# Hybrid convolution and retention layer on one core: the row factors are spread to all partitions through a DRAM row instead of by products with a unit matrix

## The chip, the core and the metric

The kernel runs on one core of one Trainium2 chip. The metric is the device time of one execution in microseconds, the median of several runs. The engines are named as the profile names them: PE (TensorE, the products), PEld (its weight loads), DVE (VectorE), ACT (ScalarE), POOL (GpSimd), and SP (SyncE, which here only issues DMAs). Each engine works through its own list of instructions in order and waits on semaphores for the others.

## The reference

One layer takes 2048 rows of 1024 numbers, with 16 learned rows ahead of them. The rows are normalised, projected to eight groups of 512, four of which go through a short gated convolution and four through a chunked retention of four heads; both results are gated, joined and projected back.

```python
def rms_norm(x, g):
    xf = x.astype(jnp.float32)
    y = xf * lax.rsqrt(jnp.mean(xf * xf, axis=-1, keepdims=True) + EPS)
    return (y * g.astype(jnp.float32)).astype(x.dtype)

def mixer_layer(h, norm_g, w_in, conv_w, ret_norm_g, w_out, pos):
    hn = rms_norm(h, norm_g)
    proj = jnp.einsum('bld,de->ble', hn, w_in)
    cx, cb, cc, cg, q, k, v, rg = jnp.split(proj, N_PROJ, axis=-1)
    conv_out = short_conv_branch(cx, cb, cc, conv_w) * jax.nn.silu(cg)
    ...
    ret = head_group_norm(retention_chunkwise(qf, kf, vf), ret_norm_g)
    ret_out = ret.astype(h.dtype) * jax.nn.silu(rg)
    mixed = jnp.concatenate([conv_out, ret_out], axis=-1)
    return h + jnp.einsum('ble,ed->bld', mixed, w_out)
```

The factor of each row, `rsqrt(mean(x*x) + EPS)`, is not multiplied into `x` ahead of the projection. The kernel projects the rows with the gain alone and multiplies the factor, or its square, into the results.

## The kernel before

**Layout.** The projections are computed transposed: output channels stand on the partitions, rows of the sequence in the free dimension. So the factor of a row is needed as a row vector that is the same on all 128 partitions. The sequence is done in two halves of 1024 rows (`for r in range(NR)`), each in two blocks of 512 (`j`). Each half goes through eight units: four convolution groups (numbers 4 to 7) and four heads (0 to 3), in the order of `UNITS`. A unit makes two groups of products. An ordinary one (`quad`, L221) takes seven products of twelve matmuls each (L232) instead of eight, with sums of blocks of the weights (`stationary`, L134, on POOL) and of `x` (`block_sums`, `prepare`). The first group after `x` changes is a plain one (`quad_plain`, L278, matmuls at L289) with no sums. After both halves eight pairs of output tiles follow.

**Two-part numbers.** Every operand of the large products is split (`split`, L107): the high half, rounded, by a cast on ACT (L110; with a scale, L113), and the low half by a subtraction on DVE (L122; with a scale, L114). Three matmuls of 128x512 make one full one: low by high, high by low, high by high. Names like `mh30`, `ml30` are the high and low half of block 3, tile 0; `wh`, `wl` are those of a weight.

**The row factors.** `row_factors(r, f)` (L387) is a generator that loads the rows of half r a second time, untransposed (L363), squares and sums them on ACT (L396), and calls `spread_factors` (L366) once for each block of 512. For half 0 it is run through ahead of the first unit; for half 1 its steps are put between the quads of units 5, 6 and 7 of half 0 (`FACTOR_STEPS`). `spread_factors` takes the factors of 512 rows as `rc`, 128 partitions by 4 (POOL's power at L305), and has `spread` (L317) bring them to all partitions as `rr`, 128 by 512, and their squares as `rr2`. `spread` multiplies a unit matrix by the factors on DVE (L310), which makes four diagonal matrices, and has PE multiply a matrix of ones by them, so that each partition receives the whole row in PSUM; ACT copies it out (L337) and squares it (L339). In half 0 that is one float32 product (L336). In half 1 the factors are split into two parts (DVE L326, L327 and ACT L330, the last for the diagonals of the high part) and two products of the rounded form are added (L332, L333). `rr` and `rr2` are read by the units of the same half, `rc2` (the squares by partition) and `ev` by the heads.

**Queues and order.** All loads and stores but a few stand in one queue, SP's. A DMA is issued when the buffer that it writes is free and what it reads is there; the DMAs behind it wait with it. Weight tiles (`ra`, L487) have eight buffers; `x`, the rows `n`, gates and other half-lived tiles share sixteen (`gen`). The order of the instructions on each engine is not the order of the code: a scheduler orders them with times of its own, so that an edit in one place can change the order far from it, within the bounds that `issue_after` and priorities set. When half 0 ends, the second group of unit 7, the split of the sixteen new `x` tiles (L409, L113, L114) and the plain first group of head 0 of half 1 overlap.

Of the kernel before, what the change touches and what calls it, by code (L numbers as in the profile page):

```python
# [8 lines left out]
F32 = mybir.dt.float32  # L9
F32R = mybir.dt.float32r  # L10
BF16 = mybir.dt.bfloat16
U16 = mybir.dt.uint16
AF = mybir.ActivationFunctionType
ALU = mybir.AluOpType

P = 128
# [6 lines left out]
HB = 512  # L23
NR = 2
BLK = SEQ // NR
CH = HB // P
# [53 lines left out]
def hybrid_trunk(ctx: ExitStack, tc: tile.TileContext, t, out: bass.AP, chunk_decay):  # L80
# [5 lines left out]
    nc = tc.nc  # L86
    x = t["x"]

    const = ctx.enter_context(tc.tile_pool(name="const", bufs=1))
    small = ctx.enter_context(tc.tile_pool(name="small", bufs=2))  # L90
    sb = ctx.enter_context(tc.tile_pool(name="sb", bufs=2))
# [6 lines left out]
    def ps_misc():  # L98
        return ps.tile([P, HB], F32, name="ms", tag="ms", bufs=4)

    def gen(name="g"):
        return sb.tile([P, HB + 16], F32, name=name, tag="g", bufs=GEN)[:, : 2 + HB]
# [18 lines left out]
    def sub(eng, out, a, b):  # L121
        eng.tensor_tensor(out=out, in0=a, in1=b, op=ALU.subtract)  # L122
# [185 lines left out]
    def diagonal(out, col, n):  # L308
        a = col.shape[1]
        nc.vector.tensor_tensor(  # L310
            out=out,
            in0=ident[:n, :n].rearrange("p (a c) -> p a c", a=1).broadcast_to([n, a, n]),
            in1=col.rearrange("p (a c) -> p a c", c=1).broadcast_to([n, a, n]),
            op=ALU.mult,
        )

    def spread(col, n, dst, squares=None, two_part=False):  # L317

        a = col.shape[1]
        diag = sb.tile([P, HB], F32R if two_part else F32, name="rot", tag="rot", bufs=1)  # L320
        diag = diag.rearrange("p (a c) -> p a c", a=CH)[:n, :a, :n]
        rp = ps_misc()
        rows = rp[:, : a * n].rearrange("p (a c) -> p a c", a=a)
        if two_part:
            high, low = (small.tile([P, CH], t, name="ch", tag=f"ch{t}")[:n, :a] for t in (F32R, F32))
            nc.vector.tensor_copy(out=high, in_=col)  # L326
            sub(nc.vector, low, col, high.bitcast(F32))  # L327
            highs = gen("dg")[:, :HB].bitcast(F32R).rearrange("p (a c) -> p a c", a=CH)[:n, :a, :n]
            for c in range(a):
                nc.scalar.mul(highs[:, c], ident[:n, :n], high[:, c : c + 1].bitcast(F32))  # L330
            diagonal(diag, low, n)
            nc.tensor.matmul(rows, ones_r[:n].broadcast_to([n, P]), highs, start=True, stop=False)  # L332
            nc.tensor.matmul(rows, ones_r[:n].broadcast_to([n, P]), diag, start=False, stop=True)  # L333
        else:
            diagonal(diag, col, n)
            nc.tensor.matmul(rows, ones[:n].broadcast_to([n, P]), diag, start=True, stop=True)  # L336
        nc.scalar.copy(out=dst, in_=rp[:, : a * n])  # L337
        if squares is not None:
            nc.scalar.activation(squares, rp[:, : a * n], AF.Square)  # L339

    gain = const.tile([P, KT], F32, name="gain")
    ident = const.tile([P, P], F32, name="ident")
    ones = const.tile([P, 1], F32, name="ones")
    ones_r = const.tile([P, 1], F32R, name="ones_r")
    neg_half = const.tile([P, CH], F32, name="neg_half")
    meta_s = const.tile([P, KT, NMETA], F32, name="meta_s")
    cols = const.tile([P, 3 * NG], F32, name="cols")
# [15 lines left out]
            nc.sync.dma_start(a, x[row : row + P, half * HB : (half + 1) * HB])  # L363
        return tiles

    def spread_factors(ss, rr, rr2, two_part):  # L366


        add(nc.vector, ss[:, 0, :], ss[:, 0, :], ss[:, 1, :])
        rc = small.tile([P, CH], F32, name="rc", tag="rc")  # L370
        v = rsqrt_mean(rc, ss[:, 0, :])
        spread(rc, P, rr, rr2, two_part)
        rc2 = small.tile([P, CH], F32, name="rc2", tag="rc2", bufs=2 * NR)
        nc.vector.tensor_tensor(out=rc2, in0=rc, in1=rc, op=ALU.mult)
        ev = small.tile([P, NG, CH], F32, name="ev", tag="ev", bufs=2 * NR)
        nc.vector.tensor_tensor(
            out=ev,
            in0=eps_col.rearrange("p (h c) -> p h c", c=1).broadcast_to([P, NG, CH]),
            in1=v.rearrange("p (h c) -> p h c", h=1).broadcast_to([P, NG, CH]),
            op=ALU.mult,  # L380
        )
        return rc2, ev

    def row_tile(name, pair):
        return sb.tile([P, BLK], F32, name=name, tag=f"rr{pair}", bufs=2)

    def row_factors(r, f):  # L387

        f.extend([row_tile("rr", r), row_tile("rr2", r), []])
        rows = load_rows(r, 0)  # L390
        yield
        for j in range(2):
            ss = small.tile([P, 2, CH], F32, name="ss", tag="ss")
            for c in range(CH):
                for half, a in enumerate(rows):
                    nc.scalar.activation(a, a, AF.Square, accum_out=ss[:, half, c : c + 1])  # L396
                if j * CH + c + 1 < 2 * CH:
                    rows = load_rows(r, j * CH + c + 1)
                yield
            f[2].append(spread_factors(ss, *(a[:, j * HB : (j + 1) * HB] for a in f[:2]), r > 0))  # L400
            yield

    def gain_of(k):
# [507 lines left out]
    make_identity(nc, ident)  # L911
    nc.gpsimd.memset(ones, 1.0)
    nc.gpsimd.memset(neg_half, -0.5)
    nc.vector.tensor_copy(out=ones_r, in_=ones)
    warm = const.tile([P, P], BF16, name="warm")
    nc.vector.memset(warm, 0.0)
    function = const.tile([P, 1], BF16, name="function")
# [21 lines left out]
    for r in range(NR):  # L939
        f = factors[r]  # L940
# [146 lines left out]
```

## Time and profile before

| | |
|---|---|
| median of 3 runs | 876.3 us (876.18 to 877.04) |
| profiled execution, span from first to last instruction | 874.9 us |
| median of the runs less that span | 1.4 us |
| PE busy | 863.1 us (99%) |
| DVE busy | 717.1 us (82%) |
| ACT busy | 474.8 us (54%) |
| POOL busy | 391.2 us (45%) |
| granted clock of PE, mean | 0.997 |
| moved by DMA | 125.32 MB, 143 GB/s on average |

In a row of the timeline stand the start in us from the span's start, the duration in us, the engine, the line of the kernel, the operation, the tiles that it writes and reads, their shapes, and, in brackets, the idle time before it with what ended it. Consecutive instructions of one kind are put together with their count. A row of the groups has count, then busy time in us and the mean of one in ns, then the idle time ahead of the group's instructions. In the rows of the queues stand KB each and the us from issue to landing. Matmuls are pipelined, so that their durations overlap and the distance of two starts is what one takes. Their shapes read "128*128 128x512": the stationary tile and the moving one.

### The profile page before, as it was taken

What the parts mean: (1) busy time and instruction counts of PE and PEld (TensorE: products, weight loads), DVE (VectorE), ACT (ScalarE), POOL (GpSimd) and SP (SyncE); (2) the same over time, 40 slices, a digit from 0 to 9 for tenths busy, and PEclk for the clock granted to TensorE, in tenths of its full rate; (3) what the DMA queues carried; (4) which work ended last, traced back from release to release, by engine and by line L of the source; (5) the groups of instructions that cost most, each with busy time, mean ns of one, the idle gap of its engine ahead of it and who ended that gap; (6) DMA issues with size and microseconds to landing.
All of it is one profiled execution on the core that took longest, in us unless ns stands there. A gap on an engine that the chain in (4) does not pass through costs nothing.

```text
span 874.9 us, 12767 instructions
## 1 busy us (share of the span) xinstructions
PE 863.1 (99%) x4280; PEld 711.8 (81%) x4280; DVE 717.1 (82%) x1190; ACT 474.8 (54%) x883; POOL 391.2 (45%) x286
## 2 busy tenths in 40 slices
PE   8999999999999999999999999999999999999996
PEld 5878788878888778888888888888888888788885
DVE  6889898989887887989889898988767799656664
ACT  8675547374644654846464646444333465545553
POOL 0662332333235555352232333354646545678763
PEclk9999999999999999999999999999999999999998
DMA  9723235353556633854243444646222594455432
GB/s 336 220 81 81 63 75 143 109 145 97 129 185 181 190 112 97 292 166 121 61 120 133 108 158 86 214 100 211 64 73 67 172 339 132 162 159 188 154 129 76
DMA packets 110321, 125.32 MB, mean 143 GB/s; under 512 B 41456, under 2 KB 58672, under 8 KB 110256
## 3 DMA queue, kind: packets, MB, share of 16 engines
q1 hardware_dynamic: 109680, 124.11, 46.9%
q8 instruction: 34, 0.56, 0.3%
q10 hardware_dynamic: 576, 0.40, 0.1%
q14 instruction: 31, 0.25, 0.1%
HBM read 90.92 MB, written 25.17 MB: 133 GB/s over the span
## 4 chain that ended last, share of the span: by engine, by line
PE 91%; DVE 5%; issue 1%; ACT 1%; DMA 1%; POOL 0%; ACTq 0%; POOLq 0%; DVEq 0%
PE pj L232 72%; PE pj L289 10%; PE ms L800 2%; PE ms L801 2%; PE ms L790 2%; PE ms L777 1%; PE ms L445 1%; DVE wl L122 1%; PE ms L768 1%; DMA ra<-in_w_in 1%; DVE ml L122 1%; DVE c L523 0%; DVE ml L114 0%; DVE rot L648 0%; DVE yo L870 0%
## 5 line engine op out<-in xcount | busy, mean ns | idle before, releaser
L232 PE MATMUL pj<-mh,wl 128*128 128x512 f32 x1008 | 397.8, 395 | 1.5 <-ACT tc L239 1.2
L232 PE MATMUL pj<-mh,wh 128*128 128x512 f32 x1008 | 393.2, 390 | 0.0
L232 PE MATMUL pj<-ml,wh 128*128 128x512 f32 x1008 | 392.5, 389 | 0.0
L110 ACT CAST wh<-ra 128x512 fp32r<-128x512 f32 x216 | 133.9, 620 | 272.5 <-PE pj L232 226.0
L122 DVE TENSOR_TENSOR wl<-ra,wh 128x512 fp32r<-128x512 f32 x216 | 188.6, 874 | 45.6 <-ACT wh L110 45.1
L232 PEld LDWEIGHTS pj<-mh,wl 128*128 128x128 f32 x1008 | 189.3, 188 | 42.7 <-issue 2.7
L232 PEld LDWEIGHTS pj<-mh,wh 128*128 128x128 f32 x1008 | 189.2, 188 | 40.1
L232 PEld LDWEIGHTS pj<-ml,wh 128*128 128x128 f32 x1008 | 189.4, 188 | 37.8
L119 POOL TENSOR_TENSOR sa<-ra 128x512 f32<-128x512 f32 x36 | 53.0, 1473 | 99.7 <-DMA ra<-in_w_in 50.9
L122 POOL TENSOR_TENSOR ra<-sa,ra 128x512 f32<-128x512 f32 x36 | 51.8, 1438 | 80.2 <-DVE wl L122 79.0
L122 POOL TENSOR_TENSOR ra<-ra 128x512 f32<-128x512 f32 x36 | 58.0, 1611 | 59.4 <-PE ms L445 47.5
L149 POOL TENSOR_TENSOR ra<-ra 128x512 f32<-128x512 f32 x36 | 61.0, 1694 | 39.5 <-issue 26.7
L239 ACT COPY tc<-pj 128x512 f32<-128x512 f32 x108 | 62.6, 580 | 0.0
L289 PE MATMUL pj<-mh,mh 128*128 128x512 f32 x128 | 51.0, 400 | 1.8 <-ACT mh L967 1.1
L289 PE MATMUL pj<-mh,ml 128*128 128x512 f32 x128 | 50.0, 390 | 0.2 <-DVE ml L122 0.2
L289 PE MATMUL pj<-ml,mh 128*128 128x512 f32 x128 | 48.1, 392 | 0.0
L813 POOL TENSOR_TENSOR rp<-rs,neg_half 128x4 f32<-128x4 f32 x16 | 17.8, 1112 | 54.8 <-DVE rs L119 54.7
L870 DVE TENSOR_TENSOR yo<-pj,yo 128x512 f32<-128x512 f32 (+1 forms) x33 | 22.0, 673 | 22.6 <-PE pj L232 15.0
L585 POOL TENSOR_TENSOR c<-c,rr 128x512 f32<-128x512 f32 x14 | 26.4, 1884 | 29.8 <-DVE c L626 18.1
L110 ACT CAST wh<-sa 128x512 fp32r<-128x512 f32 x36 | 22.2, 617 | 22.9 <-PE pj L232 22.9
L876 POOL TENSOR_TENSOR z<-yo,final_g 128x512 f32<-128x512 f32 x16 | 26.0, 1627 | 18.9 <-DVE yo L870 18.9
L817 DVE TENSOR_SCALAR pm<-ms,mv,rp 128x128 f32<-128x128 f32 x64 | 21.9, 404 | 12.4 <-POOL rp L813 12.3
(152 smaller groups left out, 1209.2 us busy)
## 6 DMA issues: line engine op xcount, KB each, us to landing
ra<-in_w_in SPq DMA_DIRECT2D x126, 256.0 KB, 2.8
x<-in_xT SPq DMA_DIRECT2D x48, 256.0 KB, 4.8
w<-in_w_out SPq DMA_DIRECT2D x32, 256.0 KB, 5.0
ra<-mixed SPq DMA_DIRECT2D x32, 256.0 KB, 2.9
yo<-in_x SPq DMA_DIRECT2D x32, 256.0 KB, 4.5
ra<-in_x SPq DMA_DIRECT2D x16, 256.0 KB, 3.6
mixed<-c SPq DMA_DIRECT2D x16, 256.0 KB, 2.4
mixed<-qg SPq DMA_DIRECT2D x16, 256.0 KB, 2.5
```

The source lines that it names most:

```text
L110: nc.scalar.copy(out=hi, in_=src)
L119: eng.tensor_tensor(out=out, in0=a, in1=b, op=ALU.add)
L122: eng.tensor_tensor(out=out, in0=a, in1=b, op=ALU.subtract)
L149: summed[0] = nc.gpsimd.tensor_tensor(out=a12, in0=a12, in1=a11, op=ALU.subtract)
L232: nc.tensor.matmul(bank, a[:, ks], b, start=first and kt == 0 and n == 0, stop=kt == KH - 1 and n == 2, skip_group_check=not first,)
L239: copied[0] = nc.scalar.copy(out=c, in_=bank)
L289: nc.tensor.matmul(banks[i], a[:, ks], b, start=half + kt + n == 0, stop=half == 1 and kt == KH - 1 and n == 2,)
L585: eng.tensor_tensor(out=out, in0=a, in1=b, op=ALU.mult)
L813: nc.gpsimd.tensor_tensor(out=rp, in0=rs, in1=neg_half.rearrange("p (c a) -> p c a", a=1), op=ALU.pow)
L817: nc.vector.tensor_scalar(out=y[:, cs], in0=o[:, cs], scalar1=mv[:, c, 0:1], scalar2=rp[:, c, :], op0=ALU.subtract, op1=ALU.mult,)
L870: last[0] = nc.vector.tensor_tensor(out=y[:, cs], in0=pp[:, cs], in1=y[:, cs], op=ALU.add)
L876: nc.gpsimd.tensor_tensor(out=ys[i][j], in0=y, in1=final_g[:, j * HB : (j + 1) * HB], op=ALU.mult)
```

## The change

`spread` is no longer used for the row factors of the two halves; it stays, cut to its float32 form, for the 16 learned rows. `spread_factors` writes `rc` to a small DRAM row (512 numbers, each its own piece, since `rc` holds four numbers on each of 128 partitions), and a second DMA reads that row back to all 128 partitions as `rr`. ACT squares `rr` from SBUF into `rr2`; the copy from PSUM goes. Both DMAs are issued by SP. There are four such rows, one for each block of 512.

```diff
-    def spread(col, n, dst, squares=None, two_part=False):
+    def spread(col, n, dst):
 
-        a = col.shape[1]
-        diag = sb.tile([P, HB], F32R if two_part else F32, name="rot", tag="rot", bufs=1)
-        diag = diag.rearrange("p (a c) -> p a c", a=CH)[:n, :a, :n]
-        rp = ps_misc()
-        rows = rp[:, : a * n].rearrange("p (a c) -> p a c", a=a)
-        if two_part:
-            high, low = (small.tile([P, CH], t, name="ch", tag=f"ch{t}")[:n, :a] for t in (F32R, F32))
-            nc.vector.tensor_copy(out=high, in_=col)
-            sub(nc.vector, low, col, high.bitcast(F32))
-            highs = gen("dg")[:, :HB].bitcast(F32R).rearrange("p (a c) -> p a c", a=CH)[:n, :a, :n]
-            for c in range(a):
-                nc.scalar.mul(highs[:, c], ident[:n, :n], high[:, c : c + 1].bitcast(F32))
-            diagonal(diag, low, n)
-            nc.tensor.matmul(rows, ones_r[:n].broadcast_to([n, P]), highs, start=True, stop=False)
-            nc.tensor.matmul(rows, ones_r[:n].broadcast_to([n, P]), diag, start=False, stop=True)
-        else:
-            diagonal(diag, col, n)
-            nc.tensor.matmul(rows, ones[:n].broadcast_to([n, P]), diag, start=True, stop=True)
-        nc.scalar.copy(out=dst, in_=rp[:, : a * n])
-        if squares is not None:
-            nc.scalar.activation(squares, rp[:, : a * n], AF.Square)
+        diag = sb.tile([P, HB], F32, name="rot", tag="rot", bufs=1)[:n, :n]
+        diagonal(diag.rearrange("p (a c) -> p a c", a=1), col, n)
+        rows = ps_misc()[:, :n]
+        nc.tensor.matmul(rows, ones[:n].broadcast_to([n, P]), diag, start=True, stop=True)
+        nc.scalar.copy(out=dst, in_=rows)
...
-    def spread_factors(ss, rr, rr2, two_part):
+    def spread_factors(ss, rr, rr2, line):
...
-        spread(rc, P, rr, rr2, two_part)
+        nc.sync.dma_start(line.rearrange("c p -> p c"), rc)
+        nc.sync.dma_start(rr, line.rearrange("c p -> (c p)").partition_broadcast(P))
+        nc.scalar.activation(rr2, rr, AF.Square)
...
+    factor_rows = {
+        (r, j): dram.tile([CH, P], F32, name=f"rc{r}{j}", tag=f"rc{r}{j}") for r in range(NR) for j in range(2)
+    }
...
-            f[2].append(spread_factors(ss, *(a[:, j * HB : (j + 1) * HB] for a in f[:2]), r > 0))
+            f[2].append(spread_factors(ss, *(a[:, j * HB : (j + 1) * HB] for a in f[:2]), factor_rows[r, j]))
```

In the changed kernel the lines below `spread` stand some 12 lines higher: the write is L355, the read L356, the squares L357, the weight loads L476 (before L487), the `x` loads L398 (before L409).

The scheduler puts other work in another order too. Three places matter for what follows, all at the end of half 0. On SP's queue, where half 0 loads the first plain weights of half 1 (`ra`) and its `x` tiles, there stood before:

```order
L487 DMA ra_3908<-in_w_in 128x512
L487 DMA ra_3914<-in_w_in 128x512
L487 DMA ra_3920<-in_w_in 128x512
L409 DMA x_3806<-in_xT 128x512
L409 DMA x_3812<-in_xT 128x512
```

and in the changed kernel, where `rc11` is the DRAM row of the second block of half 1:

```order
L476 DMA ra_3884<-in_w_in 128x512
L355 DMA rc11_89<-rc_3673 128x4x1
L356 DMA rr_2923<-rc11_89 128x512
L398 DMA x_3776<-in_xT 128x512
L398 DMA x_3782<-in_xT 128x512
```

The write and the read of the row stand ahead of the `x` loads, and the fourth weight tile has moved from ahead of the sixteen `x` loads to behind them.

On DVE, where the second group of unit 7 (`wl` are its weights) and the split of the new `x` (`ml00` to `ml13`) alternate, there stood before, behind `ml00`, up to the low half of the new head's first weight (`ml30`):

```order
L122 TENSOR_TENSOR wl_3663<-ra_3637,wh_3662 128x512
L114 SCALAR_TENSOR_TENSOR ml01_3815<-x_3812,gain_69,mh01_3814 128x512
L114 SCALAR_TENSOR_TENSOR ml02_3821<-x_3818,gain_69,mh02_3820 128x512
L114 SCALAR_TENSOR_TENSOR ml03_3827<-x_3824,gain_69,mh03_3826 128x512
L114 SCALAR_TENSOR_TENSOR ml10_3833<-x_3830,gain_69,mh10_3832 128x512
L122 TENSOR_TENSOR wl_3667<-ra_3635,wh_3666 128x512
L114 SCALAR_TENSOR_TENSOR ml11_3839<-x_3836,gain_69,mh11_3838 128x512
L122 TENSOR_TENSOR ml30_3905<-ra_3902,mh30_3904 128x512
```

and in the changed kernel, again behind `ml00` (L574 is the old L585, `tc` a gate of unit 7):

```order
L114 SCALAR_TENSOR_TENSOR ml01_3785<-x_3782,gain_69,mh01_3784 128x512
L114 SCALAR_TENSOR_TENSOR ml02_3791<-x_3788,gain_69,mh02_3790 128x512
L574 TENSOR_TENSOR tc_3670<-tc_3670,rr_374 128x512
L122 TENSOR_TENSOR wl_3646<-ra_3620,wh_3645 128x512
L114 SCALAR_TENSOR_TENSOR ml03_3797<-x_3794,gain_69,mh03_3796 128x512
L114 SCALAR_TENSOR_TENSOR ml10_3803<-x_3800,gain_69,mh10_3802 128x512
L114 SCALAR_TENSOR_TENSOR ml11_3809<-x_3806,gain_69,mh11_3808 128x512
L114 SCALAR_TENSOR_TENSOR ml12_3815<-x_3812,gain_69,mh12_3814 128x512
L122 TENSOR_TENSOR wl_3650<-ra_3618,wh_3649 128x512
L114 SCALAR_TENSOR_TENSOR ml13_3821<-x_3818,gain_69,mh13_3820 128x512
L122 TENSOR_TENSOR ml30_3875<-ra_3872,mh30_3874 128x512
```

With `ml00`, six L114 stood ahead of `ml30`, and now eight do; `tc` stood ahead of the first piece before, so it is no addition.

On PE, at the first products of the new head (`pj` are its banks; the L232 is the last of unit 7's fifth product), there stood before:

```order
L232 MATMUL pj_3674<-mh43_705,wh_3662 128x512
L289 MATMUL pj_3977<-mh00_3808,mh30_3904 128x512
L289 MATMUL pj_3977<-mh00_3808,ml30_3905 128x512
L289 MATMUL pj_3977<-ml00_3809,mh30_3904 128x512
L289 MATMUL pj_3977<-mh01_3814,mh30_3904 128x512
```

and in the changed kernel:

```order
L232 MATMUL pj_3657<-mh43_701,wh_3645 128x512
L289 MATMUL pj_3947<-mh00_3778,mh30_3874 128x512
L289 MATMUL pj_3948<-mh00_3778,mh32_3880 128x512
L289 MATMUL pj_3947<-mh00_3778,ml30_3875 128x512
L289 MATMUL pj_3947<-ml00_3779,mh30_3874 128x512
```

The product that reads `ml30` was the head's second and is its third. Elsewhere PE's list differs by the six products of the row factors that are gone and by where a few small ones (L445, L483) stand; further on, the rest of unit 7 and of the new head's products are interleaved in shorter pieces than before, in the same number.

More of the change, by code (lines that the diff above doesn't have):

```diff
@@ L343, in hybrid_trunk @@
     ones = const.tile([P, 1], F32, name="ones")
-    ones_r = const.tile([P, 1], F32R, name="ones_r")
     neg_half = const.tile([P, CH], F32, name="neg_half")
@@ L913, in hybrid_trunk @@
     nc.gpsimd.memset(neg_half, -0.5)
-    nc.vector.tensor_copy(out=ones_r, in_=ones)
     warm = const.tile([P, P], BF16, name="warm")
```

## The prediction

> **What bounds the kernel now.** I read the page first, then the groups by line, then the timeline of TensorE at each place that the change touches, then the queues. The span and the busy times:
>
> ```profile
> span 874.9 us, 12767 instructions
> PE 863.1 (99%) x4280; PEld 711.8 (81%) x4280; DVE 717.1 (82%) x1190; ACT 474.8 (54%) x883; POOL 391.2 (45%) x286
> ```
>
> TensorE (PE) works almost without a pause, so a product that goes is worth its time only if what stands behind it on PE is ready earlier too. The median of the runs shown is 876.3 us, 1.4 above this span; I make the sum against 874.9 and add the 1.4 at the end. About 0.2% (1.75 us) is what a measurement of this kernel can tell from no change: faster means below 874.55, slower above 878.05.
>
> **What the change takes off PE.** Before, four row factors were spread by products: in the first half by one float32 product each (L336), in the second by two products of the rounded form each (L332, L333). The timeline of PE around the two of the first half:
>
> ```profile
> 44.16 0.39 PE L289 MATMUL pj<-ml,mh 128*128 128x512 f32 x1
> 44.39 1.02 PE L336 MATMUL ms<-rot,ones 128*128 128x512 f32 x2
> 44.84 0.79 PE L289 MATMUL pj<-mh,mh 128*128 128x512 f32 x1
> 45.47 0.39 PE L289 MATMUL pj<-mh,ml 128*128 128x512 f32 x1
> ...
> 50.27 0.39 PE L289 MATMUL pj<-mh,ml 128*128 128x512 f32 x1
> 50.50 1.02 PE L336 MATMUL ms<-rot,ones 128*128 128x512 f32 x2
> 51.45 0.23 PE L483 MATMUL ms<-ident,mk 16*128 16x16 f32 x1
> 51.61 1.07 PE L445 MATMUL ms<-ra,meta_s 128*16 128x128 f32 x32
> ```
>
> The durations overlap (products are pipelined), so I count from start to start. An ordinary product of 512 columns takes 0.23 us of PE (50.27 to 50.50). From 44.16 to 45.47 are 1.31 us, in which two ordinary ones would take 0.45: the first L336 costs 0.86. The second holds PE from 50.50 to 51.45, 0.95. L483, which stood right behind it, moves ahead and then stands alone between other products; no row of these shows what that costs, it lies between nothing and the 0.86 that the far larger L336 costs alone, and I take 0.2, a little over its 0.16 (51.45 to 51.61). So the first half gives 0.86 + 0.95 - 0.2 = 1.6. The groups and the timeline of the second half:
>
> ```profile
> L332 PE MATMUL ms<-dg,ones_r 128*128 128x512 f32 x2 | 0.8, 392 | 0.0
> L333 PE MATMUL ms<-rot,ones_r 128*128 128x512 f32 x2 | 0.8, 392 | 0.0
> ```
>
> ```profile
> 359.63 0.39 PE L232 MATMUL pj<-mh,wh 128*128 128x512 f32 x1
> 359.86 0.40 PE L332 MATMUL ms<-dg,ones_r 128*128 128x512 f32 x1
> 360.09 0.40 PE L333 MATMUL ms<-rot,ones_r 128*128 128x512 f32 x1
> 360.33 0.39 PE L232 MATMUL pj<-mh,wl 128*128 128x512 f32 x1
> ```
>
> A pair takes 0.47 (359.86 to 360.33), two pairs 0.9. PE is relieved of 1.6 + 0.9 = 2.5 us. PE waited for none of these products' inputs (idle 0.0 in the groups), so nothing more goes with them. VectorE loses the diagonals and the splitting into two parts, ScalarE the copies out of PSUM and eight scalings; neither sets the end where they stood; the cast of the column of ones at the start is 128 values, nothing.
>
> **What the change adds.** On SyncE's queue, which does everything in turn, stand four writes of 512 values of 4 bytes and four reads of the 2 KB row by 128 partitions. A write waits there for GpSimd's power (L305), the read for the write's landing, and every later load waits behind both. Who waits for those loads: the weights' split (ScalarE L110, VectorE L122) and then PE. The trace has no such write. The nearest rows of the queues' view, with KB and us from issue to landing:
>
> ```profile
> mixed<-c SPq DMA_DIRECT2D x16, 256.0 KB, 2.4
> ...
> final_g<-in_final_g SPq DMA_DIRECT2D x1, 512.0 KB, 4.4
> ...
> cols<-in_cols SPq DMA_DIRECT2D x1, 6.0 KB, 6.7
> ```
>
> `mixed` goes to DRAM in 512 runs of 512 bytes, the same number of pieces as the new write, and lands in 2.4; `cols` (128 pieces of 48 bytes, queued behind a 1 MB load) took 6.7. I take 2.4 for the write where the queue is empty, as it is nearest to `mixed` in the number of pieces and the direction, and keep 6.7 as the far end; below 2.4 nothing would change, since the read is not what is waited for then. The read is like `final_g`, half as large: 2.8 to 4.4. The Trainium skill, page DMA: Bandwidth & Descriptors, section Specifications, says that transfers under 512 bytes are done as read-modify-write, and its section on the anatomy of one DMA that most of the fixed time is the receipt of the write, longest for HBM. No run here shows a 4-byte write; by that rule the far end would be the nearer one, and the sum 876.5 instead of 875.3 (both are worked out below, from the rows).
>
> In the first half the write is ready when GpSimd's L305 ends, and the weights it can delay are four tiles, the last of them issued here, with its us to landing from the queues' view of that moment:
>
> ```profile
> 36.81 1.03 POOL L305 TENSOR_TENSOR rc<-rs_v,neg_half 128x4 f32<-128x4 f32 x1 [4.42 <-DVE rs_v L302]
> ...
> 41.49 0.33 SPq L487 DMA_DIRECT2D ra<-in_w_in  x1
> ```
>
> ```profile
> ra<-in_w_in SPq DMA_DIRECT2D x1, 256.0 KB, 5.9
> ```
>
> At 37.84 the power is done and SyncE is about to issue the last `x` rows, whose landings lag like this one by some 6 us; so the write is issued at about 38.2 and lands at about 44.2, behind the loads ahead of it. The fourth weight tile then goes out at 44.6 instead of 41.49 and lands between 47.4 (2.8 behind its issue) and 50.5 (5.9). PE reads it in L445, now at 51.61 - 1.6 = 50.0. That is a stall of nothing to 0.5; I take nothing. The second factor of that half holds up weights of the head's second group of products (L751) only, which comes a whole first group of 84 products, 84 x 0.23 = 19 us, later.
>
> In the second half, second factor:
>
> ```profile
> 346.56 1.02 POOL L305 TENSOR_TENSOR rc<-rs_v,neg_half 128x4 f32<-128x4 f32 x1 [3.72 <-DVE rs_v L302]
> ...
> 353.84 0.42 SPq L409 DMA_DIRECT2D x<-in_xT  x1
> ```
>
> L305 ends at 347.58, 2.05 earlier with what PE has been relieved of by then (1.6 and one pair): 345.5. The write lands at 345.6 + 2.4 = 348.0, and the sixteen `x` loads, which stood behind one more weight tile and began at 353.84, follow right behind the read, at about 348.4. They come earlier, not later. What they feed is the next stage's start, and here the new order of the work matters more than the queue.
>
> **Where the gain is given back.** VectorE in the stretch in which unit 7 ends and the next head begins:
>
> ```profile
> 355.21 2.08 DVE L510 SCALAR_TENSOR_TENSOR c<-u,conv_w,c 128x512 f32<-128x512 f32 x3 [0.31 <-ACT c L508]
> ...
> 360.72 2.73 DVE L114 SCALAR_TENSOR_TENSOR ml<-x,gain,mh 128x512 fp32r<-128x512 f32 x4
> 363.37 0.68 DVE L122 TENSOR_TENSOR wl<-ra,wh 128x512 fp32r<-128x512 f32 x1
> 363.97 1.78 DVE L114 SCALAR_TENSOR_TENSOR ml<-x,gain,mh 128x512 fp32r<-128x512 f32 x1
> 365.68 0.68 DVE L122 TENSOR_TENSOR ml<-ra,mh 128x512 fp32r<-128x512 f32 x1
> ```
>
> From 355.21 on VectorE has no idle time; it is full up to the low half of the new head's first weight (ml30, at 365.68). PE at that moment:
>
> ```profile
> 365.80 0.39 PE L289 MATMUL pj<-mh,mh 128*128 128x512 f32 x1
> 366.41 0.50 PE L289 MATMUL pj<-mh,ml 128*128 128x512 f32 x1 [0.22 <-DVE ml L122]
> 366.75 0.40 PE L289 MATMUL pj<-ml,mh 128*128 128x512 f32 x1
> ```
>
> PE waits for exactly this ml30 already: its second product of the head starts at 366.41 instead of 366.03. So here the two engines arrive together, and any work put ahead of ml30 is paid for. The order of the changed program puts two more L114 ahead of it (ml12 and ml13; eight instead of six), because the `x` tiles come sooner in it. One costs 0.66 in a row (360.72 to 363.37 for four): 1.33. VectorE's full stretch starts with what PE releases, so it begins 2.05 earlier; ml30 ends at 366.36 - 2.05 + 1.33 = 365.64. The changed order lets two products of the head go ahead that don't need it, and the third, which does, starts at about 365.7, where it started at 366.75. PE arrives at 365.80 - 2.5 + 0.46 = 363.8 and waits 1.9. Of 2.5 us 1.05 is left, and behind this stretch the order is PE's own: the same number of products follows. The span becomes 874.9 - 1.05 = 873.85, the time 873.85 + 1.4 = 875.3. If VectorE's delays in that row (1.78 against 0.66, 1.1 us) fall otherwise, it is 1.1 better or as much worse: 874.2 to 876.4.
>
> **Rivals.** First, the whole gain: the delays of VectorE fall behind ml30, or the added L114 run while it would have been idle; then PE keeps 2.5 and loses the old wait of 0.38 as well: 873.4, and with a part of the wait up to 874.5. For it speaks that VectorE is relieved of two diagonals just ahead; against it that it waits for PE, not for them, at the start of the stretch (0.31 behind ScalarE's L508).
>
> Second, slower: the write of 4-byte pieces lands late. In the second half ScalarE's squares (L357) stand ahead of the first `x` tile on that engine and need the read. In the old place stood:
>
> ```profile
> 356.00 1.28 ACT L330 ACTIVATE dg<-ident,ch 128x128 fp32r<-128x128 f32 x4
> 357.18 0.71 ACT L113 ACTIVATE mh<-x,gain 128x512 fp32r<-128x512 f32 x1
> ```
>
> The square comes at 356.00 - 2.05 = 353.95. The read lands at 345.6 + W + 2.8 for a write that takes W, so W up to 5.5 is hidden, and each further us delays ScalarE, VectorE's full stretch and PE by as much. At the far end, 6.7, the time is 875.3 + 1.2 = 876.5, with the longer read (4.4) 878.1, at the edge. With a read of 2.8 slower begins at W = 8.3. At 9 the second half loses 3.5, and in the first half the fourth weight tile lands at 38.2 + 9 + 0.4 + 2.8 = 50.4, 0.4 late: 879.2. Against it speaks that nothing in the trace takes 9 us to land. The skill's read-modify-write rule, named above, is the one by which it would.
>
> Third, nothing is left: a stall of 0.5 at L445 and VectorE at its worse end use up the 2.5: 876.3 to 877.
>
> **How the numbers follow.** The forecast (0.42) and the third rival (0.09) lie within 0.2%; of the first rival (0.37) all is faster; the second (0.12) is slower. The forecast's own range is 874.2 to 876.4, so a small part of it is faster, and about as much of the first rival could end just within the bound: faster 0.37, same 0.51, slower 0.12. From 873.4 (first rival) to 877.0 (third rival's end) lie nearly nine in ten by these chances, and the slower case is left out; the ends are those of the unknown costs above, and I see no reason to draw them closer.
>
> **What would show it.** Right: L336 at 512 columns, L332 and L333 are gone, PE's starts between 57 and 355 us come 1.6, then 2.05 earlier, and the third product of the new head waits for VectorE's ml of the weights by 1.5 to 2 us. Wrong: a write that takes over 5.5 us to land with the squares (L357) or an L113 waiting for a DMA; L445 waiting for a weight load near 50 us; or no wait of PE at the new head, with the span near 872.

## The result and the profile after

The changed kernel takes 903.1 us (median of 4 runs, 900.4 to 903.6) against 876.3 (4 runs, 876.18 to 877.04): a ratio of 1.0295, with an interval of 1.0282 to 1.0309, 26.8 us slower. Its profiled execution has a span of 901.5 us. The head of its page:

```profile
span 901.5 us, 12745 instructions
PE 870.0 (97%) x4272; PEld 715.9 (79%) x4272; DVE 710.8 (79%) x1181; ACT 471.2 (52%) x871; POOL 393.8 (44%) x286
```

Eight matmul rows have gone (the six products of the row factors; a float32 one counts as two), and yet PE is busy for 7 us longer and idle for 31.5 us instead of 11.8. The landing times of the new write, and the waits of the whole run that name the new instructions or what stands behind them (columns: us in all, times, the longest):

```profile
DMA to landing us min/median/max: 9.0/10.0/10.4
```

```profile
ACT rr L357 <- DMA rr<-rc: 24.5, 3, 9.4
...
PE pj L232 <- ACT tc L239: 12.4, 3, 6.7
...
PE ms L434 <- DMA ra<-in_w_in: 9.9, 2, 6.1
```

The write takes 9.0 to 10.4 us, not 2.4. One of the three waits for L239 (1.2 us) is in the kernel before too. SyncE's queue around the two factors of the first half, where the fourth weight tile (L476) used to go out at 41.49:

```profile
38.01 0.40 SPq L355 DMA_DIRECT2D rc<-rc  x1
...
39.05 1.61 SPq L476 DMA_DIRECT2D ra<-in_w_in  x3
48.47 0.33 SPq L356 DMA_DIRECT2D rr<-rc  x1
48.92 0.35 SPq L476 DMA_DIRECT2D ra<-in_w_in  x1
51.51 0.38 SPq L355 DMA_DIRECT2D rc<-rc  x1
```

The write was issued at 38.0, as forecast at 38.2. The read waits at the head of the queue till 48.47, and the tile behind it goes out at 48.92 instead of the 44.6 that I had worked out. PE stops four times in the run, once for each factor; the last product ahead of each stop and the first behind it:

```profile
49.23 0.39 PE L289 MATMUL pj<-mh,ml 128*128 128x512 f32 x1
53.41 1.12 PE L434 MATMUL ms<-ra,meta_s 128*16 128x128 f32 x32 [3.79 <-DMA ra<-in_w_in]
...
65.64 0.39 PE L232 MATMUL pj<-mh,wh 128*128 128x512 f32 x1
70.53 0.50 PE L232 MATMUL pj<-mh,wl 128*128 128x512 f32 x1 [4.51 <-ACT tc L239]
...
328.88 0.39 PE L232 MATMUL pj<-mh,wh 128*128 128x512 f32 x1
335.37 1.01 PE L434 MATMUL ms<-ra,meta_s 128*16 128x128 f32 x10 [6.10 <-DMA ra<-in_w_in]
...
381.14 0.39 PE L232 MATMUL pj<-mh,wh 128*128 128x512 f32 x1
388.24 0.80 PE L232 MATMUL pj<-mh,wl 128*128 128x512 f32 x1 [6.71 <-ACT tc L239]
388.83 0.63 PE L232 MATMUL pj<-ml,wh 128*128 128x512 f32 x1
389.26 0.63 PE L232 MATMUL pj<-mh,wh 128*128 128x512 f32 x1
```

From start to start, less the 0.23 of an undisturbed product, the stops cost 3.95 + 4.66 + 6.26 + 6.87 = 21.7 us. The last two lines show a second cost: behind each stop a product takes 0.43 us (388.83 to 389.26) instead of 0.23. The windows of the fourth stop and of the 4 us behind it (length; busy time of each engine; then PE's granted clock, DMA share, GB/s):

```profile
381.20:388.00 6.80, 0.33 (x2) 0.00 (x0) 5.08 (x8) 6.46 (x11) 0.00 (x0) 0.81 1.05 396
388.00:392.00 4.00, 3.76 (x9) 3.00 (x10) 4.00 (x6) 4.00 (x9) 2.04 (x1) 0.50 1.05 387
```

The granted clock is 0.50 there. Six to nine products at 0.2 us more each follow every stop; with the slower ones at both ends of that stretch it is 1.6 to 2.9 us a stop, some 8 us in the four places. 21.7 + 8 less the 2 to 2.5 that the removed products were worth is 27.2 to 27.7, about one more than the difference of the spans, 26.6 (901.5 - 874.9); where that one comes back was not followed.

The second stop is the plainest. ScalarE at that place:

```profile
65.23 0.63 ACT L357 ACTIVATE rr<-rr 128x512 f32<-128x512 f32 x1 [9.38 <-DMA rr<-rc]
...
69.88 0.60 ACT L239 COPY tc<-pj 128x512 f32<-128x512 f32 x1
```

ScalarE stands for 9.38 us at the squares, and the copy out of PSUM (L239) that PE needs is behind them.

### The profile page after: what moved, and what is told of

Its sections match the earlier page's. It is cut to its first block, busy times and chain, and to the rows that moved or that the text cites. A ratio compares the mean times of both kernels' runs of the same rounds, so it can differ in the third digit from the quotient of the medians.

```text
span 901.5 us, 12745 instructions
## 1 busy us (share of the span) xinstructions
PE 870.0 (97%) x4272; PEld 715.9 (79%) x4272; DVE 710.8 (79%) x1181; ACT 471.2 (52%) x871; POOL 393.8 (44%) x286
## 4 chain that ended last, share of the span: by engine, by line
PE 80%; DVE 4%; DMA 4%; ACT 2%; issue 1%; POOL 1%; SPq 0%; POOLq 0%; ACTq 0%; DVEq 0%
PE pj L232 67%; PE pj L289 5%; DMA rc<-rc 2%; PE ms L789 2%; PE ms L790 2%; PE ms L779 1%; PE ms L766 1%; PE ms L434 1%; DMA x<-in_xT 1%; PE ms L757 1%; DVE wl L122 1%; DMA ra<-in_w_in 1%; DVE ml L122 0%; DMA n<-in_x 0%; DVE c L512 0%
## 5 line engine op out<-in xcount | busy, mean ns | idle before, releaser
L232 PE MATMUL pj<-mh,wl 128*128 128x512 f32 x1008 | 400.6, 397 | 12.7 <-ACT tc L239 12.4
L232 PE MATMUL pj<-mh,wh 128*128 128x512 f32 x1008 | 395.1, 392 | 0.0
L232 PE MATMUL pj<-ml,wh 128*128 128x512 f32 x1008 | 394.8, 392 | 0.0
L232 PEld LDWEIGHTS pj<-mh,wl 128*128 128x128 f32 x1008 | 190.6, 189 | 55.8 <-ACT tc L239 13.6
L232 PEld LDWEIGHTS pj<-mh,wh 128*128 128x128 f32 x1008 | 190.6, 189 | 40.4
L232 PEld LDWEIGHTS pj<-ml,wh 128*128 128x128 f32 x1008 | 190.8, 189 | 38.5
L119 POOL TENSOR_TENSOR sa<-ra 128x512 f32<-128x512 f32 x36 | 54.9, 1525 | 108.7 <-DMA ra<-in_w_in 38.2
L122 POOL TENSOR_TENSOR ra<-ra 128x512 f32<-128x512 f32 x36 | 55.2, 1532 | 55.8 <-PE ms L434 47.2
L149 POOL TENSOR_TENSOR ra<-ra 128x512 f32<-128x512 f32 x36 | 57.6, 1601 | 31.8 <-issue 18.3
L239 ACT COPY tc<-pj 128x512 f32<-128x512 f32 x108 | 62.6, 580 | 0.1
L574 POOL TENSOR_TENSOR c<-c,rr 128x512 f32<-128x512 f32 x14 | 28.8, 2057 | 29.3 <-DVE c L615 18.0
L110 ACT CAST wh<-sa 128x512 fp32r<-128x512 f32 x36 | 22.3, 618 | 27.2 <-PE pj L232 27.2
L114 DVE SCALAR_TENSOR_TENSOR ml<-x,gain,mh 128x512 fp32r<-128x512 f32 x32 | 25.8, 838 | 12.0 <-ACT mh L113 11.9
```

The source lines that it names most:

```text
L110: nc.scalar.copy(out=hi, in_=src)
L114: nc.vector.scalar_tensor_tensor(out=lo, in0=src, scalar=scale, in1=hi.bitcast(F32), op0=ALU.mult, op1=ALU.subtract)
L119: eng.tensor_tensor(out=out, in0=a, in1=b, op=ALU.add)
L149: summed[0] = nc.gpsimd.tensor_tensor(out=a12, in0=a12, in1=a11, op=ALU.subtract)
L232: nc.tensor.matmul(bank, a[:, ks], b, start=first and kt == 0 and n == 0, stop=kt == KH - 1 and n == 2, skip_group_check=not first,)
L239: copied[0] = nc.scalar.copy(out=c, in_=bank)
```

## The experiments

Three things were open: why the write takes 10 us, by which way that reaches PE (the queue, ScalarE's order, or the transfers themselves), and whether the rest of the forecast, above all the gain given back at the new head, holds once the write is fast. Each time is set against runs of the kernel before that were taken beside it, 876.7 us in most and 877.05 in the last.

### A chain of writes by themselves

Behind the last stores of the changed kernel stands a chain on SyncE's queue: a write to DRAM, then a read of one number of it that waits for the landing and that the next write waits for.

```diff
+        def link(name, shape, view, src, first):
+            d = dram.tile(shape, F32, name=name, tag=name)
+            with tc.issue_after(stored[0].ins):
+                nc.sync.dma_start(view(d), src)
+                stored[0] = nc.sync.dma_start(s[0:1, 0:1], first(d))
```

> The changed kernel with a chain of small writes to DRAM behind its last stores, each followed by a read of one number that the next write waits for, so that each stands alone; only the landing times are read. Theory A (pieces that share a short stretch of DRAM are rewritten one after the other): 512 pieces of 4 bytes side by side take 9 to 10 us, the same 512 pieces 64 or 512 bytes apart under 4 us, 128 pieces of 16 bytes side by side still 5 or more. Theory B (each piece costs, wherever it lies): all three of 512 pieces take 9 to 10 us, 128 pieces (of 16 or of 4 bytes) about 4 us, 32 pieces and one piece about 2 us. Theory C (any write of pieces shorter than 512 bytes pays a fixed 7 us more): even 32 pieces and the single piece of 4 bytes take about 9 us, and 128 or 4 pieces of 512 bytes 2 to 3 us. Theory D (the write was slow only because other loads ran): all take under 4 us here.

Rows of SyncE's queue; from the issue of a write to that of its read is what the write takes:

```profile
902.43 0.40 SPq L841 DMA_DIRECT2D qb<-s  x1
904.34 0.23 SPq L842 DMA_DIRECT2D s<-qb  x1
...
908.42 0.35 SPq L841 DMA_DIRECT2D qd<-s  x1
909.84 0.24 SPq L842 DMA_DIRECT2D s<-qd  x1
911.50 0.34 SPq L841 DMA_DIRECT2D qe<-s  x1
918.96 0.24 SPq L842 DMA_DIRECT2D s<-qe  x1
...
927.68 0.21 SPq L841 DMA_DIRECT2D qg<-s  x1
928.71 0.21 SPq L842 DMA_DIRECT2D s<-qg  x1
...
939.39 0.39 SPq L841 DMA_DIRECT2D qz<-s  x1
949.60 0.21 SPq L842 DMA_DIRECT2D s<-qz  x1
```

512 pieces of 4 bytes side by side (`qz`) take 10.2 us with nothing else under way: theory D falls. The same 512 pieces 64 bytes apart (`qb`) take 1.9: B falls. One piece of 4 bytes (`qg`) takes 1.0: C falls. 128 pieces of 4 bytes side by side (`qe`) take 7.5, but 128 of 16 bytes (`qd`) only 1.4, where A expected 5 or more. So A holds for pieces of 4 bytes that lie side by side, and not for those of 16. The time doesn't grow in step with the number of pieces: 32 side by side take 2.9 us, 128 take 7.5 and 512 take 10.2.

### Distances, sizes, and a load behind the write

The same chain with other distances; then with a 256 KB load of `x` issued behind the write.

```diff
+        link("pa", [CH, P], side, four)
+        link("pb", [CH, P, 2], apart, four)
...
+        link("la", [1, 1], None, None, nc.sync)
+        link("lb", [CH, P], side, four, nc.sync)
+        link("lc", [P, CH], lambda d: d, four, nc.sync)
+        link("ld", [CH, P], side, four, nc.scalar)
+        link("le", [CH, P, 16], apart, four, nc.sync)
```

> The changed kernel with a second chain of writes behind its last stores, each alone; only times of the chain are read. First 512 pieces of 4 bytes at distances of 4, 8, 16, 32 and 64 bytes, 128 pieces of 8 bytes, 128 and 64 of 4 bytes. Then a load of 256 KB alone, and the same load issued right behind 512 pieces of 4 bytes side by side, behind 128 of 16 bytes, behind the 4-byte pieces but from ScalarE's queue, and behind 512 pieces 64 bytes apart. Theory A' (pieces of 4 bytes that share one short stretch of DRAM wait for one another, and what follows the write in the DMA engines waits with it): about 10 us at 4 bytes, falling with the distance to about 2 at 64; 128 pieces of 8 bytes 2 to 7; the load alone takes 3 to 4 us, 8 us or more behind the side-by-side pieces, 3 to 5 behind the others. Rival 1 (the load is only slow where it is issued from the same queue): behind the pieces but from ScalarE's queue it takes 3 to 5 us. Rival 2 (a load passes the write): 3 to 5 us everywhere.

By the time from the issue of a write to that of its read, 512 pieces of 4 bytes take 9.1, 4.2, 2.6, 2.1 and 1.8 us at 4, 8, 16, 32 and 64 bytes; the one at 8 bytes as rows:

```profile
905.29 0.40 SPq L845 DMA_DIRECT2D pb<-s  x1
909.50 0.23 SPq L855 DMA_DIRECT2D s<-pb  x1
```

Side by side, 128 pieces of 8 bytes take 2.7, 128 of 4 bytes 6.9 and 64 of 4 bytes 6.6. The load alone takes at most 2.9 us, 4.5 behind the 16-byte pieces, 3.2 behind those 64 bytes apart. Behind the 4-byte pieces side by side the queues' view has it at

```profile
s<-in_x SPq DMA_DIRECT2D x1, 256.0 KB, 11.9
```

and from ScalarE's queue it is the same. The load of that link went out at 965.73 and its reader at 977.50, 11.8 later; what the DMA engines moved between, in 40 slices:

```profile
GB/s 0 0 6 64 62 49 0 28 14 14 14 7 7 28 7 7 7 14 21 14 21 14 7 14 21 7 0 14 21 0 14 14 21 14 7 7 139 181 21 0
```

After a first stretch of about 1 us at 49 to 64 GB/s the load trickles at 28 GB/s or less, and nearly 40% of it moves in the last us (139 and 181 GB/s). The view gives no landing for this write. It was issued at 965.43, and alone it takes 9.1 to 10.2 us, so it would be done between 974.5 and 975.6; the load speeds up at 976.3. Both rivals fall: the slow write holds up the load behind it on the DMA engines, from either of the two queues tried. The Trainium skill, page DMA: Bandwidth & Descriptors, section Queues, rings and completion order, says that a semaphore is raised only after every earlier write of the same DMA engine, across its queues; the landing at 11.9 agrees, though here the data itself is late too.

### The writes alone, side by side and apart

The kernel before, products and all; the four writes are added, and nothing reads them. The second of the two spaces the pieces.

```diff
         spread(rc, P, rr, rr2, two_part)
+        nc.sync.dma_start(line.rearrange("c p -> p c"), rc)
```

```diff
-        nc.sync.dma_start(line.rearrange("c p -> p c"), rc)
+        nc.sync.dma_start(line[:, :, 0].rearrange("c p -> p c"), rc)
...
-        (r, j): dram.tile([CH, P], F32, name=f"rc{r}{j}", tag=f"rc{r}{j}") for r in range(NR) for j in range(2)
+        (r, j): dram.tile([CH, P, 16], F32, name=f"rc{r}{j}", tag=f"rc{r}{j}") for r in range(NR) for j in range(2)
```

> The kernel before, products and all, with the four writes of 512 numbers added and nothing that reads them. Theory 1 (the write costs only through what waits for its landing): 875.5 to 877.5 us, though each write still lands 9 to 10 us after its issue. Rival (the small pieces slow the other transfers while they are under way): 880 us or more, with the loads beside the writes landing some us later than before.

> As the kernel with the four writes alone (the kernel before, products and all, and nothing reads the rows), but the 512 pieces of 4 bytes of a write lie 64 bytes apart. Number, size and order of the pieces are the same. Theory A' (the cost is that pieces side by side wait for one another): 876 to 877.5 us, as the kernel before. Rival (the cost is that there are 512 small pieces): about 885 us, as with the pieces side by side.

Side by side: 885.3 us against 876.7, a ratio of 1.0103 (1.0087 to 1.0120). Apart: 877.1 against 876.7, 1.0007 (0.9998 to 1.0016). My theory for the first missed: a write that nobody waits for costs 8.6 us. The lines of landing, first of side by side, then of apart:

```profile
DMA to landing us min/median/max: 9.9/10.3/10.6
```

```profile
DMA to landing us min/median/max: 1.9/2.2/5.3
```

The weight loads beside the first write in the two, and in the kernel before, all in the stretch from 37.2 to 47.2 us:

```profile
ra<-in_w_in SPq DMA_DIRECT2D x6, 256.0 KB, 9.8
```

```profile
ra<-in_w_in SPq DMA_DIRECT2D x7, 256.0 KB, 5.6
```

```profile
ra<-in_w_in SPq DMA_DIRECT2D x7, 256.0 KB, 5.9
```

The loads behind the dense write land 4 us later; in the chain it was 9. With pieces of the same number, size and order, 64 bytes apart, the cost is gone. How a write that nobody waits for stops PE: the load of the last `x` rows is issued right behind it, ScalarE waits 2.96 us for that load (L401), and the second factor of the half, which needs its sums, is late. With the dense pieces, the largest single wait of PE is

```profile
PE ms L336 <- DVE rot L310: 3.0, 1, 3.0
```

for the diagonals of that factor. A second one, of 1.9 us for L239, comes at the end of half 0, where the kernel before has none; the rest of the 8.6 us lies in smaller waits and was not followed.

### Rows that nobody uses

The kernel with the writes alone, and a read that brings 64 numbers of each row to an unused tile; what is left of the change is the queue.

```diff
+        unused = sb.tile([P, CH * CH * CH], F32, name="unused", tag="unused", bufs=1)
+        nc.sync.dma_start(unused, line.rearrange("c p -> (c p)")[: CH * CH * CH].partition_broadcast(P))
```

> The kernel before, products and all, with the four writes and four reads added; a read brings 64 numbers of the row to a tile that nobody uses (the factors still come from the products). What is left of the change is the wait in SyncE's queue. Theory 1 (both the queue behind the read and ScalarE's squares cost): 882 to 888 us: PE waits 3 to 5 us at the meta products for the fourth weight tile and some 3 to 5 us at the start of half 1 for the x tiles, and not in the two other places. Rival (the queue alone costs everything): 900 us or more. Rival (ScalarE alone does): 875.5 to 877.5 us.

890.4 us, a ratio of 1.0155 (1.0131 to 1.0179; the runs spread from 887.1 to 892.4): 13.7 us, more than I expected and half of the loss. PE has two long stops in the profile, which is that of the fastest run:

```profile
54.44 1.12 PE L336 MATMUL ms<-rot,ones 128*128 128x512 f32 x2 [2.99 <-DVE rot L310]
...
370.99 0.80 PE L232 MATMUL pj<-mh,wl 128*128 128x512 f32 x1 [3.67 <-DVE ml L114]
```

The second is the one that theory 1 named, at the start of half 1. The first is not: PE does not wait there for the fourth weight tile but for the diagonals of the second factor, as with the writes alone, and any wait for the tile is hidden behind it. So 8.6 of the 13.7 us are the writes' own, which theory 1 had left out; what the queue adds to them is some 5 us, of which the slow products behind the two stops are a part. Both rivals fall. The read here is an eighth of the real one, so that the real queue may well cost more.

### The squares later

The changed kernel, with both squares of a half moved to where their rows are long there.

```diff
-        nc.scalar.activation(rr2, rr, AF.Square)
+        squares.append(lambda: nc.scalar.activation(rr2, rr, AF.Square))
...
+    def square(n):
+        with tc.issue_after(copied[0].ins):
+            for _ in range(n):
+                squares.pop(0)()
...
         def complete():
+            square(2)
...
             def rest_of_sums():
+                square(2)
```

> The changed kernel, writes and reads as they are, but the squares of the rows (L357) stand later on ScalarE, where their row has long arrived: both of half 0 at the completion of the first unit, both of half 1 in the first head. Theory 1 (the part of the loss that the queue doesn't explain is ScalarE waiting in its order at L357): the two waits of PE for ScalarE's copies (4.5 and 6.1 us, with the slow products behind them some 16 us in all) go, and the time is 885 to 890 us. Rival (the late rows are waited for by others, or the queue costs all): 897 us or more.

896.3 us, 6.8 less than the changed kernel, between the two expectations and nearer to the rival's. Of the two stops that ScalarE's copies ended (4.51 and 6.71 us; the 6.1 of the expectation is the third stop's) one goes, that at 65 us: there ScalarE's order was what cost. The first stays (3.90), and so does the third, with ScalarE out of it:

```profile
323.12 0.39 PE L232 MATMUL pj<-mh,wh 128*128 128x512 f32 x1
329.36 1.01 PE L441 MATMUL ms<-ra,meta_s 128*16 128x128 f32 x10 [5.85 <-DMA ra<-in_w_in]
```

It is a weight tile behind the read in SyncE's queue. The fourth fell only from 6.71 to 5.61 us idle. There the `x` tiles behind the read are nearly as late as the squares were (ScalarE waited 6.89 us for those):

```profile
375.07 2.05 ACT L113 ACTIVATE mh<-x,gain 128x512 fp32r<-128x512 f32 x3 [6.51 <-DMA x<-in_xT]
```

In both kernels seven such L113 stand ahead of the L239 that PE waits for.

### Pieces of 16 bytes

The changed kernel with the DRAM row in the order of the partitions; ScalarE puts the row in order when it has arrived.

```diff
-        nc.sync.dma_start(line.rearrange("c p -> p c"), rc)
-        nc.sync.dma_start(rr, line.rearrange("c p -> (c p)").partition_broadcast(P))
+        nc.sync.dma_start(line, rc)
+        nc.sync.dma_start(rr2, line.rearrange("p c -> (p c)").partition_broadcast(P))
+        nc.scalar.copy(
+            out=rr.rearrange("q (c p) -> q c p", c=CH), in_=rr2.rearrange("q (p c) -> q c p", c=CH)
+        )
         nc.scalar.activation(rr2, rr, AF.Square)
...
-        (r, j): dram.tile([CH, P], F32, name=f"rc{r}{j}", tag=f"rc{r}{j}") for r in range(NR) for j in range(2)
+        (r, j): dram.tile([P, CH], F32, name=f"rc{r}{j}", tag=f"rc{r}{j}") for r in range(NR) for j in range(2)
```

> The changed kernel with the DRAM row in the order of the partitions: a write is 128 pieces of 16 bytes instead of 512 of 4, the read is the same 2 KB row to all partitions, and ScalarE puts it in order by a copy before it squares it (half a us more for each). Theory B (each piece costs): the write lands in about 4 us, the waits of PE shrink by some 6 us in each place, and the time falls to 876 to 882 us. Theories A and C: the write still takes 7 us or more and the time stays at 897 us or above.

876.25 us against 876.71, a ratio of 0.9993 (0.9984 to 1.0003): all of the loss is gone, and so is nearly all of the gain. Theories A and C fall. The time lies within theory B's range, but by luck: B had the write at 4 us, and the chain had ruled it out. The write's landing, and PE at the new head:

```profile
DMA to landing us min/median/max: 1.4/2.1/6.1
```

```profile
364.41 0.61 PE L289 MATMUL pj<-mh,mh 128*128 128x512 f32 x2
365.94 0.50 PE L289 MATMUL pj<-mh,ml 128*128 128x512 f32 x1 [0.91 <-DVE ml L122]
```

This is close to the case that the prediction describes, but for the order of the pieces and ScalarE's copy: a write of 2.1 (the first of the four 6.1, issued at 38.21, as forecast), two products of the head that go ahead, and a third that waits for VectorE's ml30, at 365.94 where the prediction has 365.7.

### The weights' low halves first

The kernel of the 16-byte pieces, and ml30, ml31 and ml32 made ahead of ml12 and ml13; and, as a control, the same order in the kernel before.

```diff
-            m, b = moving(load_x(r), gain_of)
-            first = [plain_parts(w_loads(0))]
...
+            m, b = moving(load_x(r), gain_of, {(0, 5): lambda: weights(0, 2), (0, 7): lambda: weights(1, 3)}, {(0, k): first_low for k in (6, 7)})
+            first = [w]
```

> The kernel with the 16-byte pieces, and at the start of half 1 VectorE makes the low halves of the head's first weights (ml30, ml31, ml32) ahead of two low halves of x (ml12, ml13) instead of behind them; nothing else is moved. Theory (the gain of the removed products is given back there, by 1.33 us of VectorE's work ahead of ml30): PE's wait of 0.91 us for ml30 goes, and the time is 0.8 to 1.3 us lower than without: 875.0 to 875.5 us. Rival (another engine arrives as late): 876.0 us or more, with PE waiting for something else within the first ten products of the head.

> The control for the last kernel: the kernel before, products and all, with the same order at the start of half 1 (ml30, ml31 and ml32 ahead of ml12 and ml13). In the kernel before ml30 stands there already, so only ml31 and ml32 move up. Theory (the gain of the last kernel is that of the removed products, kept): 876.0 to 877.0 us, no difference from the kernel before that can be told. Rival (the order alone brings it): 875.0 us or less.

> The kernel with 16-byte pieces and the low halves of the weights first, once more, beside the control: 874.2 to 875.2 us, below the control by 1.5 to 2.5 us, if the removed products' 2 us of TensorE is kept; within 0.5 us of the control if the order alone was it.

874.6 us against 876.7, a ratio of 0.9975 (0.9965 to 0.9984); once more, beside the control, 874.9 against 877.05, 0.9975 (0.9966 to 0.9984); the control 877.3, 1.0002 (0.9993 to 1.0011). At the head PE no longer waits:

```profile
364.27 0.39 PE L292 MATMUL pj<-mh,mh 128*128 128x512 f32 x1
364.54 0.50 PE L292 MATMUL pj<-mh,ml 128*128 128x512 f32 x1
364.88 0.39 PE L292 MATMUL pj<-ml,mh 128*128 128x512 f32 x1
```

The first is 0.4 us below the lowest that I expected. The order alone brings nothing that can be told. In the control PE still waits at the head, for an ml30 that VectorE begins at 366.04 (363.05 in the kernel without the products):

```profile
366.77 0.50 PE L292 MATMUL pj<-mh,ml 128*128 128x512 f32 x1 [0.88 <-DVE ml L113]
```

With the row through DRAM in 16-byte pieces and the new order the gain is kept, 2.1 us. This version beats both kernels.

## Why the prediction was wrong

**The step that failed** is the duration W of the write, "I take 2.4 for the write ..., as it is nearest to `mixed` in the number of pieces and the direction". It took 9.0 to 10.4. The number of pieces was the wrong likeness: `mixed` has pieces of 512 bytes, and 512 pieces of 4 bytes take 1.8 us 64 bytes apart and 10.2 side by side. What counted in these runs is that small pieces are neighbours in DRAM. The far end, 6.7, was too near as well, for `cols` is a read of DRAM, and the argument against the slower rival ("nothing in the trace takes 9 us to land") was only that the trace held no such write. The rule of the Trainium skill that the prediction names for it (page DMA: Bandwidth & Descriptors, section Specifications: read-modify-write under 512 bytes) did point to the right side, but not to the right line: 16-byte pieces are under 512 too and take 1.4 us.

**The price of a late write** was the second error. The rival's mechanism was right, but it allowed 0.4 us in the first half and 3.5 in the second at W = 9, 879.2 in all: 2.9 of the 26.8 us that the change cost. In the two places that it priced, the sizes were wrong. It took 2.8 us for what lands behind the write. The read of the fourth stop took 6.0; with that its own sum gives 9.0 + 6.0 - 8.35 = 6.65 us (8.35 is 353.95 less 345.6), and the stop was 6.71 idle. In the first stop the write took 10.4 for its 9, and the weight tile behind the read 4.4 for its 2.8.

Other terms are missing. It took the loads between write and read as untouched, but a load behind the dense write lands 4 us later (the writes alone cost 8.6 us). It said that the second factor of the first half holds up weights only for a group 19 us later, and left out that ScalarE stands at L357 there (4.51 us idle, gone with the late squares). It did not price the first factor of half 1 at all, where a weight tile stands behind the read (6.10 us idle). And each stop costs 1.6 to 2.9 us more in slow products, which no part of the prediction had. "W up to 5.5 is hidden" was worked out for one factor of four.

**What held.** The write's place and issue in the first half (38.0 for 38.2). That PE is relieved, though by 2.0 rather than 2.5. The same two large products, one at the start and one at the end of unit 7, in the kernel before (the later one is in the prediction, at 360.33) and in the one with the low halves first:

```profile
6.99 0.50 PE L289 MATMUL pj<-mh,mh 128*128 128x512 f32 x1 [1.13 <-ACT mh L967]
```

```profile
6.75 0.50 PE L292 MATMUL pj<-mh,mh 128*128 128x512 f32 x1 [0.89 <-ACT mh L961]
...
358.08 0.39 PE L235 MATMUL pj<-mh,wl 128*128 128x512 f32 x1
```

The later one comes 2.25 us earlier, 0.24 of which were there from the start. The gain given back at the head, which the forecast rested on: with a fast write it is there, at the product and by the engine that were named, and taking two L114 from ahead of ml30 gives it back. The waiting was 0.91 us and not 1.9, since PE was ready for it at 364.87 (two products of 0.23 from 364.41) instead of 363.8: of the 1.1 us, 0.5 are the smaller gain, and 0.46 a wait for ScalarE's L239 shortly ahead (at 361.56), which I had not foreseen. For a write of 2.1 us the forecast's own range of 874.2 to 876.4 holds what was measured, 876.25. But that is 0.46 us below the kernel before, measured beside it, and no difference that can be told, where the forecast was 1.05; the range was wide enough for both.

**What stays open.** That the pieces are rewritten one after the other in the memory is a reading that fits the distances, but no run looks into the memory, and in its simplest form it doesn't fit the numbers (2.9, 6.6, 7.5 and 10.2 us for 32, 64, 128 and 512 pieces). In the fourth stop of the changed kernel late squares and late `x` tiles hide one another: with the squares moved away 5.61 of 6.71 us stay, and no run made the tiles early and left the squares. In the kernel with 16-byte pieces ScalarE works without a pause from 353.04 up to the L239 that PE waits for, and the copy and the square of the row (1.1 and 0.6 us) stand in that stretch; whether the wait goes without them was not tried.

## What to carry to other kernels

A column of single numbers, one to a partition, should not be written side by side to DRAM: keep the partition's own run together (16 bytes were enough here), or space the pieces, and put the order right on an engine after the read. Price a transfer by its pieces and where they land, not by its bytes or by their number, and count a slow one against the loads issued behind it, from another queue too, even if nobody waits for it. Where nothing in a profile resembles a new transfer, its far end is not the slowest row that happens to be there, and each place where it is waited for has to be priced, not the nearest one alone.

## What the runs showed of the hardware that I had not expected

Writes of 4 bytes side by side take 2.9 us for 32 of them, 6.6 for 64, 6.9 and 7.5 for 128, and 9.1 to 10.2 for 512 by themselves; at a distance of 16 bytes 512 take 2.6. Behind such a write a 256 KB load mostly gets 28 GB/s or less and takes 11.9 us instead of at most 2.9.

Every pause of PE from 2.99 us up, in the three kernels looked at for it (the changed one, that with the unused rows and that with the late squares), was followed by 3.6 to 5.8 us of slow products at a granted clock of about 0.5; behind the pause of 4.51 us this began 0.8 us after PE went on. In the kernel with the writes alone a pause of 2.95 us had no such price. The Trainium skill, page TensorE: Matmul & The Clock Gate, section Part 1: The HAM clock gate (the "warmup" mystery), gives about 3.4 us of idleness for the clock to fall and about as long for it to come back; the slow stretches here are 0.2 to 2.4 us longer than the second, and in the kernel with the unused rows a pause of 2.99 us, a little less than the first, was enough.
